# A decoder trunk on one core: chunks share first-projection weights, squares are summed in pairs, convolution taps are laid out anew, the norms' order is fixed, and half of the normed tiles stay in PSUM

## The chip, the cores and the metric

The kernel runs on one core of a Trainium2 chip. The metric is the device time of one execution in microseconds (us), given as the median of several runs. TensorE (PE in the rows) has a granted clock of 1.0 (2.4 GHz) or 0.5 (1.2 GHz) in the rows. VectorE is DVE, ScalarE is ACT, GpSimd is POOL, and SyncE is SP, which issues the DMAs.

## What is computed

The whole trunk is one launch, for 1024 tokens of width 1024 in float32:

```python
for layer in range(2):
    if layer == 0:   h = h + conformer_conv(h, ...)
    else:            h = h + nsa_attention(h, ..., kv)
    h = h + swiglu_ffn(h, ...)                 # (silu(gate) * up) @ w_out, behind an rmsnorm
    if layer == 0:   kv = shared_kv(h, ...)    # keys and values, computed once
return rmsnorm(h, final_norm)

def conformer_conv(x, ...):
    a, b = split(rmsnorm(x) @ pw1_w + pw1_b, 2)          # first projection
    h = a * sigmoid(b)
    h = depthwise causal convolution of 31 taps (h) + dw_b
    h = silu(layernorm(h))
    return h @ pw2_w + pw2_b                             # second projection
```

Attention takes softmax(score - slope * distance), with a mask, over three branches (compressed, selected and window), weighted by gates.

## The kernel before

The tokens are held in two chunks, c = 0 and 1, of 512 each (T), and each of the 1024 columns lies on partitions, in 8 tiles (KT) of 128x512. Matrix products keep float32 accuracy by three matmuls: each operand is split into a high part (yh, wh) and a low part (yl, wl), and `mm3` (L137) issues wh·yh, wh·yl and wl·yh for each of the 8 tiles k. A split (L177, L179) is a copy on ACT (yh) and a subtraction on DVE or POOL (yl). Weights come by one DMA of 512 KB, a copy on ACT (L158) and a subtraction on POOL (L160).

**First projection.** `pw1_tile(c, j)` fills two PSUM tiles, the value and its gate, with 24 matmuls each; `pw1_out` multiplies both by the norm's factor in chunk 0 (L361, L362), and makes u (L371) from the gate's tanh. So the norm's factor comes after the projection in chunk 0, and ahead of it in chunk 1 (`norm_y`, L272, makes the normed tile, and the split follows).

**Convolution.** Each tile of u has 31 taps. n1 of them go through ACT (product cv, L328) and POOL (sum zb, L329), n2 through PE as a diagonal matrix dgw (L319, L320, two passes each), and DVE takes the rest, one instruction each (L332), into a PSUM tile. The sum with zb is z (L336), and z is added up over the tiles in acc (L343).

**Norms.** Squares are added up on DVE or POOL into one tile acc (L190), and four column matmuls with ones (L201, in pieces called statistics below) give the sums of squares. Ten DVE instructions on 128x4 (L252 to L262) take the inverse root, a diagonal dg (L213) is made of it, and one matmul with ones (L220) spreads it over the partitions. The layernorm takes the mean first (`centre`, L382), and its squares of chunk 0 aren't added up: each of the eight goes to four statistics of its own. `normal` multiplies z (L401), takes the silu on ACT (L403) and splits.

**What sets the order.** PE's order is written by hand. `go(g, time)` runs the generator g of matmuls for so long, and `sides` holds the statistics, one of which goes behind each matmul of `mm3`. The tiles of the first projection of chunk 1 are the filler `fill` that PE runs while the layernorm of chunk 0 and the norm behind it are worked out. The other engines' orders come from a scheduler; `behind(g, rate)` runs the convolution beside the main generator, and `mark` and `later` add edges of order. Each engine runs its own list in order. PSUM has 8 banks here for `mm_ps()`, of one tile each; normed tiles lie in them where `roomy` is set, and so take the banks that the next matmuls need.

```python
        for k in range(KT):
            t = self.mm_ps() if self.roomy and k not in pool else self.tmp("yt")
            nc.vector.scalar_tensor_tensor(t, self.h[c][k], ..., r, OP.mult, OP.mult)
            y.append(split(t, k) if split else self.split(t, "pool" if k in pool else "dve"))
```

Of the kernel before, what the change touches and what calls it, by code (L numbers as in the profile page):

```python
# [37 lines left out]
NEG = -1e30  # L38
# [36 lines left out]
TAPS = (9, 4), (10, 0)  # L75
TAPS_END = (5, 6)
# [4 lines left out]
RATE0 = 1.05  # L81
# [17 lines left out]
PRINT = 0  # L99
YB = 16  # L100


class Net:
# [23 lines left out]
    def mm3(self, ps, w, y, kts, start=True, stop=True):  # L127
# [6 lines left out]
        for a, k in enumerate(kts):  # L134
            yh, yl = y[k]
            for b, (x, y_) in enumerate(((wh, yh), (wh, yl), (wl, yh))):
                nc.tensor.matmul(ps, x[:, a, :], y_, start=start and a + b == 0,  # L137
                                 stop=stop and a == n - 1 and b == 2)
                if self.sides:
                    self.sides.pop(0)()  # L140
# [32 lines left out]
    def split(self, src, lo="dve"):  # L173
# [3 lines left out]
        nc.scalar.activation(yh, src, AF.Copy)  # L177
# [4 lines left out]
    def sumsq(self, c, k, src, eng, pool=None):  # L182
# [4 lines left out]
        else:  # L187
            sq = pool.tile([128, T], F32, name="sq", tag="b") if pool else self.tmp("sq")
            nc.scalar.activation(sq, src, AF.Square)
            eng.tensor_tensor(self.acc[c], self.acc[c], sq, OP.add)  # L190
# [74 lines left out]
    def norm_y(self, c, vcol, split=None, pool=(), kept=False):  # L265
# [3 lines left out]
        y = []  # L269
        for k in range(KT):  # L270
            t = self.mm_ps() if self.roomy and k not in pool else self.tmp("yt")
            nc.vector.scalar_tensor_tensor(t, self.h[c][k], self.vec[:, vcol + k:vcol + k + 1],  # L272
                                           r, OP.mult, OP.mult)
            y.append(split(t, k) if split else self.split(t, "pool" if k in pool else "dve"))
        return y
# [15 lines left out]

    def later(self, ins):
# [9 lines left out]
    def conv_tile(self, c, j):  # L302
# [5 lines left out]
        n1, n2 = TAPS_END if c == 0 and j == KT - 1 else TAPS[c]  # L308
# [28 lines left out]
        if j == 0:  # L337
            self.acc[c] = z
        else:
            old = self.acc[c]  # L340
            if j == 1:
                self.acc[c] = self.cp.tile([128, T], F32, name="acc", tag="acc", bufs=2)
# [10 lines left out]
    def pw1_out(self, c, j, r=None):  # L353
# [5 lines left out]
        a = self.tmp("a")  # L359
        if r is not None:  # L360
            nc.vector.tensor_tensor(th, pb, r, OP.mult)  # L361
            nc.vector.tensor_tensor(a, pa, r, OP.mult)  # L362
            pa, pb = a, th
# [5 lines left out]
        else:  # L369
            nc.scalar.activation(u[:, 0:CW - 1], self.u[c - 1][j][:, T:T + CW - 1], AF.Copy)  # L370
        nc.vector.scalar_tensor_tensor(u[:, CW - 1:], th, 1.0, a, OP.add, OP.mult)  # L371
        self.u[c][j] = u

    def pw1_tile(self, c, j, r=None):
        yield from self.pw1_mm(c, j, self.y[c])
        self.pw1_out(c, j, r)

# [16 lines left out]
    def normal(self, c):  # L394
# [4 lines left out]
        y = []  # L399
        for j in range(KT):  # L400
            self.later(nc.vector.tensor_tensor(z[j], z[j], r, OP.mult))  # L401
            s = self.tmp("si") if c or j in LNP[c] else self.mm_ps()
            nc.scalar.activation(s, z[j], AF.Silu, bias=self.vec[:, V_LNB + j:V_LNB + j + 1],  # L403
                                 scale=self.vec[:, V_LNG + j:V_LNG + j + 1])
            y.append(self.split(s, "pool" if j in LNP[c] else "dve"))
        if c == 0:
            self.mark(self.last)
        self.yln[c] = y

    def layernorm(self, c):  # L410

        yield 4.0
        self.centre(c)
        yield 10.0
        self.sides.extend(self.rstd_parts([self.acc[c]]))
        yield 6.0
        while self.sides:
            yield 1.0
        self.rstd_spread(c, True)
# [408 lines left out]
    def q_tile(self, j, c):  # L828
# [4 lines left out]
        for g in range(2):  # L833
            a = slice(g * DH, (g + 1) * DH)
            b = slice((1 - g) * DH, (2 - g) * DH)
            f = DH ** -0.5 / SLOPE[g * HG + j]
# [65 lines left out]
    def bias_base(self):  # L902
# [3 lines left out]
        for (c0, w, step, off) in ((0, S, 1, 896), (BT_WIN, 640, 1, 512),  # L906
                                   (BT_CMP, 119, 16, 896 - (LC - 1))):
            nc.gpsimd.iota(b[:, c0:c0 + w], pattern=[[step, w]], base=-off,
                           channel_multiplier=-1, allow_small_or_imprecise_dtypes=True)
            nc.gpsimd.affine_select(out=b[:, c0:c0 + w], in_=b[:, c0:c0 + w],  # L910
                                    pattern=[[-step, w]], compare_op=OP.is_ge, fill=NEG,
                                    base=off, channel_multiplier=1)
        nc.gpsimd.affine_select(out=b[:, BT_WIN:BT_WIN + 640], in_=b[:, BT_WIN:BT_WIN + 640],
                                pattern=[[1, 640]], compare_op=OP.is_ge, fill=NEG,
# [34 lines left out]
    def scores(self, out, K, q, g, head, i, win):  # L949


        nc = self.nc
# [18 lines left out]
        for a in range(m):  # L971
# [5 lines left out]
            for e, (br, p0, pn, b0) in enumerate(segs):  # L977
# [7 lines left out]
                init = mx[:, prev[e]:prev[e] + 1] if e in prev else -3.0e38  # L985
# [556 lines left out]
```

## Time and profile before

| | before |
|---|---|
| time, median of 3 runs | 2627.57 us (2625.74 to 2631.69) |
| the profiled execution: time, span | 2629.18 us, 2627.5 us |
| mean granted clock of TensorE | 0.981 |
| busy: PE, DVE, ACT, POOL | 2512.0 us (96%), 1765.8 us (67%), 1291.6 us (49%), 1469.2 us (56%) |
| PE matmuls | 12946 |
| weights of the first projection | 46 DMAs of 512 KB, those of the second projection included |

PE is busy nearly all of the span, so a gain must come from fewer matmuls, from its waits, or from the stretches at half clock. The profile's groups are sums over stages: the waits have to be looked up where they fall. A row of the timeline shows the start, the length, the engine, the line, output and inputs, and in brackets how long the engine was idle before it and what ended that.

### The profile page before, as it was taken

Reading aid. Unit: us, or ns where it says so; the run is one execution under the profiler, and the core shown is the slowest. Engines: PE = TensorE matmul, PEld = TensorE weight load, DVE = VectorE, ACT = ScalarE, POOL = GpSimd, SP = SyncE. Lnnn points to the kernel's source line nnn. Section 1 sums busy time; section 2 is a strip of 40 time slices with the busy share of each in tenths; the row PEclk is TensorE's granted clock in tenths of the full one; section 3 lists DMA queues with packets and bytes.
Section 4 is the critical chain, followed back from the end, with each engine's and each line's share of the span. In section 5 each row is a group of like instructions: output and inputs, shape, how many; then the busy total and the mean of one; then the engine's idle time right before and its main releaser. Section 6 shows DMA issues by size and latency. Waiting matters only on the chain. (4 is left out here: it accounts for less than half of the span.)

```text
span 2627.5 us, 37191 instructions
## 1 busy us (share of the span) xinstructions
PE 2512.0 (96%) x12946; PEld 2083.5 (79%) x12946; DVE 1765.8 (67%) x3652; ACT 1291.6 (49%) x2517; POOL 1469.2 (56%) x1156
## 2 busy tenths in 40 slices
PE   8898899999799999999999999999999999899997
PEld 6676788888677878887878788888888887698986
DVE  6995788677774556665556566667666655777775
ACT  6555554444534554555543355555555543334444
POOL 8794889666543554555543354535445433566664
PEclk9999899999899999999999999999999999999999
DMA  4222223232446222322355531213212124143332
GB/s 163 72 73 66 80 81 97 88 93 92 152 146 190 87 89 62 112 86 82 90 161 167 190 101 45 81 44 108 70 53 74 54 78 158 58 129 97 97 95 75
DMA packets 111212, 258.29 MB, mean 98 GB/s; under 512 B 17265, under 2 KB 28848, under 8 KB 111024
## 3 DMA queue, kind: packets, MB, share of 16 engines
q1 hardware_dynamic: 111024, 255.91, 31.0%
q8 instruction: 102, 1.67, 0.3%
q14 instruction: 86, 0.70, 0.1%
HBM read 226.37 MB, written 29.42 MB: 97 GB/s over the span
## 5 line engine op out<-in xcount | busy, mean ns | idle before, releaser
L160 POOL TENSOR_TENSOR wl<-wr,wh 128x1024 fp32r<-128x1024 f32 (+2 forms) x396 | 740.6, 1872 | 661.1 <-ACT wh L158 625.1
L137 PE MATMUL mm<-yh,wh 128*128 128x512 f32 x1424 | 595.4, 418 | 31.7 <-DVE yl L179 30.4
L137 PE MATMUL mm<-yl,wh 128*128 128x512 f32 x1424 | 567.6, 399 | 5.0 <-DVE yl L179 5.0
L137 PE MATMUL mm<-yh,wl 128*128 128x512 f32 x1424 | 566.2, 398 | 1.8 <-POOL wl L160 1.8
L158 ACT ACTIVATE wh<-wr 128x1024 fp32r<-128x1024 f32 (+2 forms) x396 | 332.5, 840 | 426.3 <-PE mm L137 287.1
L137 PE MATMUL mm<-gh,wh 128*128 128x512 f32 x1360 | 439.4, 404 | 1.8 <-ACT gh L592 1.4
L137 PEld LDWEIGHTS mm<-yh,wh 128*128 128x128 f32 x1424 | 272.1, 191 | 86.3 <-DVE yl L179 32.1
L137 PEld LDWEIGHTS mm<-yh,wl 128*128 128x128 f32 x1424 | 271.3, 191 | 63.5 <-POOL wl L160 2.2
L137 PEld LDWEIGHTS mm<-yl,wh 128*128 128x128 f32 x1424 | 272.6, 191 | 49.5 <-DVE yl L179 6.2
L1030 DVE TENSOR_TENSOR pl<-pt,ph 128x512 fp32r<-128x512 f32 (+3 forms) x320 | 206.4, 646 | 149.6 <-ACT ph L1029 148.7
L137 PEld LDWEIGHTS mm<-gh,wh 128*128 128x128 f32 x1360 | 243.3, 189 | 48.8 <-issue 3.5
L137 PE MATMUL mm<-gh,wl 128*128 128x512 f32 x680 | 270.0, 397 | 3.7 <-POOL wl L160 3.7
L1029 ACT ACTIVATE ph<-pt 128x512 fp32r<-128x512 f32 (+3 forms) x320 | 178.7, 559 | 177.6 <-PE pt L1026 175.2
L1000 POOL TENSOR_SCALAR PS<-PS,sm,gates 128x31 f32<-128x31 f32 (+9 forms) x256 | 154.7, 615 | 191.4 <-DVE sm L997 164.6
L332 DVE SCALAR_TENSOR_TENSOR mm<-u,vec,mm 128x512 f32<-128x512 f32 x306 | 225.6, 752 | 8.0 <-PE mm L320 1.8
L995 ACT ACTIVATE PS<-PS,mx 128x31 f32<-128x31 f32 (+9 forms) x256 | 139.5, 546 | 115.6 <-DVE mx L993 115.3
L329 POOL TENSOR_TENSOR zb<-zb,cv 128x512 f32<-128x512 f32 x132 | 178.8, 1355 | 14.4 <-ACT zb L314 8.8
L1000 POOL TENSOR_SCALAR PW<-PW,sm,gates 128x640 f32<-128x640 f32 (+4 forms) x128 | 96.2, 752 | 155.1 <-DVE sm L997 131.8
L606 DVE TENSOR_TENSOR h<-mm,h 128x512 f32<-128x512 f32 x184 | 124.7, 684 | 81.7 <-PE mm L137 81.3
L137 PEld LDWEIGHTS mm<-gh,wl 128*128 128x128 f32 x680 | 128.0, 188 | 37.7 <-POOL wl L160 7.5
L995 ACT ACTIVATE PW<-PW,mx 128x640 f32<-128x640 f32 (+4 forms) x128 | 88.8, 694 | 101.2 <-DVE mx L993 100.5
L507 PE MATMUL mm<-y,wh 128*128 128x256 f32 x1008 | 133.8, 286 | 2.3 <-DVE wh L492 1.9
(243 smaller groups left out, 4814.4 us busy)
## 6 DMA issues: line engine op xcount, KB each, us to landing
wr<-in_fin_dram SPq DMA_DIRECT2D x176, 512.0 KB, 3.3
wr<-in_fout_dram SPq DMA_DIRECT2D x128, 256.0 KB, 2.7
wr<-in_pw_dram SPq DMA_DIRECT2D x46, 512.0 KB, 3.3
wr<-in_fout_dram SPq DMA_DIRECT2D x64, 192.0 KB, 2.4
wr<-in_wq_dram SPq DMA_DIRECT2D x16, 512.0 KB, 4.0
qd<-q SPq DMA_DIRECT2D x32, 256.0 KB, 2.2
qt<-qd SPq DMA_DIRECT2D x32, 256.0 KB, 2.8
wr<-in_wo_dram SPq DMA_DIRECT2D x16, 512.0 KB, 3.7
```

Of the source, the lines that this page charges most:

```text
L137: nc.tensor.matmul(ps, x[:, a, :], y_, start=start and a + b == 0, stop=stop and a == n - 1 and b == 2)
L158: nc.scalar.activation(wh[:, :kt, :cols], wr[:, :kt, :cols], AF.Copy)
L160: e.tensor_tensor(wl[:, :kt, :cols], wr[:, :kt, :cols], wh[:, :kt, :cols].bitcast(F32), OP.subtract)
L329: nc.gpsimd.tensor_tensor(zb, zb, t, OP.add)
L332: later(nc.vector.scalar_tensor_tensor(ps, u[:, w:w + T], dw(w), ps, OP.mult, OP.add))
L507: nc.tensor.matmul(ps, u[:, a], v, start=a + b == 0, stop=a == n - 1 and b == 2)
L606: self.nc.vector.tensor_tensor(h, ps, h, OP.add)
L995: nc.scalar.activation(P[:, p0:p0 + pn], P[:, p0:p0 + pn], AF.Exp, bias=mx[:, e:e + 1], accum_out=sm[:, e:e + 1])
L1000: nc.gpsimd.tensor_scalar(P[:, p0:p0 + pn], P[:, p0:p0 + pn], sm[:, e:e + 1], self.gates[:, i, gt:gt + 1], OP.mult, OP.mult)
L1029: nc.scalar.activation(ph[:rows, :width], pt[:rows, :width], AF.Copy)
L1030: nc.vector.tensor_tensor(pl[:rows, :width], pt[:rows, :width], ph[:rows, :width].bitcast(F32), OP.subtract)
```

## The change

- Tiles j = 4 to 7 of the first projection load their weights once for both chunks (`pw1_pair`); chunk 1 is then taken in the order 4, 5, 6, 7, 3, 2, 0, 1.
- In the first two norms squares are added in pairs on POOL (three pairs, and two tiles alone: 5 tiles, 20 statistics in place of 4); those of the first norm go back to back on PE, not between matmuls. The layernorm of chunk 0 has 20 statistics in place of 32. In eight other norms the last squared tile ("sl") isn't added but gets 4 statistics of its own. In all there are 128 statistics, 76 before.
- PE's taps (dgw) go from 34 to 22; POOL's products go from 132 to 140; DVE's taps go from 306 to 310.
- `pw1_out` works in place in PSUM. A copy of each tile's last 30 columns (halo) is kept for chunk 1.
- `norm_y` puts only even tiles into PSUM, and edges of order hold a multiplication back until the split of two tiles before is done (AHEAD); `normal` gets such edges as well.
- In the attention the scores' sign is turned, so that 256 small DVE instructions (TENSOR_SCALAR on 128x1 or 128x2) fall away.

```diff
-TAPS = (9, 4), (10, 0)
-TAPS_END = (5, 6)
+TAPS = (10, 2), (10, 0)
+TAPS_FIRST, TAPS_END = (11, 0), (5, 10)
-RATE0 = 1.05
+RATE0 = 0.85
+AHEAD = 2
+WARM = 4.0
+ORDER1 = (4, 5, 6, 7, 3, 2, 0, 1)
...
+    def paired(self, sq):
+        for k in range(0, KT - 2, 2):
+            self.nc.gpsimd.tensor_tensor(sq[k], sq[k], sq[k + 1], OP.add)
+        return sq[0:KT - 2:2] + sq[KT - 2:]
...
-        self.sides.extend(self.rstd_parts(tiles or [self.acc[c]]))
+        self.sides.extend(self.rstd_parts(tiles or [self.acc[c], self.sq[c]]))
...
-            t = self.mm_ps() if self.roomy and k not in pool else self.tmp("yt")
+            t = self.mm_ps() if self.roomy and k % 2 == 0 and k not in pool else self.tmp("yt")
...
+            if len(low) >= AHEAD:
+                self.order(ins, low[-AHEAD])
...
-            nc.vector.tensor_tensor(th, pb, r, OP.mult)
-            nc.vector.tensor_tensor(a, pa, r, OP.mult)
-            pa, pb = a, th
+            nc.vector.tensor_tensor(pb, pb, r, OP.mult)
+            nc.vector.tensor_tensor(pa, pa, r, OP.mult)
...
+    def pw1_pair(self, j):
+        w = self.wload(self.pw1[j], 8), self.wload(self.pw1[8 + j], 8)
+        for c in range(NC):
+            yield from self.pw1_mm(c, j, self.y[c], w)
+            self.pw1_out(c, j, None if c else self.rs[0])
...
+            if len(low) > AHEAD:
+                self.order(ins, low[-1 - AHEAD])
...
+            if len(high) >= AHEAD:
+                self.order(ins, high[-AHEAD])
...
-        self.rstd(1, g)
-        go(g, 2 * TILE)
+        g = pairs()
+        self.rstd(1, g, sq1)
         self.y[1] = self.norm_y(1, V_ANORM)
         go(g)
-        fill = every(self.pw1_tile, range(KT), 1)
-        go(fill, HOLD * 2 * TILE)
+        fill = every(self.pw1_tile, ORDER1[KT - 4:], 1)
+        go(fill, 4 * TILE)
         self.rest()
-        go(fill, 2.0)
         sq = self.centre(0)
-        go(fill, 6.0)
-        self.rstd(0, fill, sq)
+        go(fill, WARM)
+        self.per = 2
+        self.rstd(0, fill, self.paired(sq))
+        self.per = 1
```

At three places this is what the engines' lists become. The first is DVE at the layernorm of chunk 0, from the first product z·r on. Before, all eight products stand ahead of the first split (mm_1875 and so on are silu tiles in PSUM):

```order
L401 TENSOR_TENSOR z_414<-z_414,mm_1872 128x512
L401 TENSOR_TENSOR z_550<-z_550,mm_1872 128x512
...
L401 TENSOR_TENSOR z_1295<-z_1295,mm_1872 128x512
L401 TENSOR_TENSOR z_1427<-z_1427,mm_1872 128x512
L179 TENSOR_TENSOR yl_1878<-mm_1875,yh_1877 128x512
L179 TENSOR_TENSOR yl_1885<-mm_1882,yh_1884 128x512
L179 TENSOR_TENSOR yl_1892<-mm_1889,yh_1891 128x512
```

After the change, at the same place:

```order
L442 TENSOR_TENSOR z_427<-z_427,mm_1891 128x512
L442 TENSOR_TENSOR z_651<-z_651,mm_1891 128x512
L442 TENSOR_TENSOR z_799<-z_799,mm_1891 128x512
L183 TENSOR_TENSOR yl_1897<-mm_1894,yh_1896 128x512
L442 TENSOR_TENSOR z_951<-z_951,mm_1891 128x512
L183 TENSOR_TENSOR yl_1904<-mm_1901,yh_1903 128x512
L442 TENSOR_TENSOR z_1086<-z_1086,mm_1891 128x512
L183 TENSOR_TENSOR yl_1911<-mm_1908,yh_1910 128x512
L442 TENSOR_TENSOR z_1250<-z_1250,mm_1891 128x512
L183 TENSOR_TENSOR yl_1918<-mm_1915,yh_1917 128x512
```

Products and splits now alternate. PE's filler waits for the split yl_1892 (the third) before and for yl_1918 (the fourth) after.

The second place is DVE at the norm ahead of the keys and values of chunk 0 (V_KVN), six products into PSUM before, with four of the next norm (yt) behind them and ahead of the splits:

```order
L272 SCALAR_TENSOR_TENSOR mm_6305<-h0_97,vec_88,mm_6277 128x512
L272 SCALAR_TENSOR_TENSOR mm_6311<-h0_98,vec_88,mm_6277 128x512
L272 SCALAR_TENSOR_TENSOR yt_6695<-h0_93,vec_88,rs_6279 128x512
L272 SCALAR_TENSOR_TENSOR yt_6700<-h0_94,vec_88,rs_6279 128x512
L272 SCALAR_TENSOR_TENSOR yt_6705<-h0_95,vec_88,rs_6279 128x512
L272 SCALAR_TENSOR_TENSOR yt_6710<-h0_96,vec_88,rs_6279 128x512
```

After the change:

```order
L292 SCALAR_TENSOR_TENSOR mm_6245<-h0_94,vec_88,mm_6241 128x512
L292 SCALAR_TENSOR_TENSOR yt_6251<-h0_95,vec_88,mm_6241 128x512
L199 TENSOR_TENSOR acc_6193<-acc_6193,sq_6297 128x512
L183 TENSOR_TENSOR yl_6248<-mm_6245,yh_6247 128x512
L292 SCALAR_TENSOR_TENSOR mm_6257<-h0_96,vec_88,mm_6241 128x512
L183 TENSOR_TENSOR yl_6254<-yt_6251,yh_6253 128x512
L292 SCALAR_TENSOR_TENSOR yt_6263<-h0_97,vec_88,mm_6241 128x512
L183 TENSOR_TENSOR yl_6260<-mm_6257,yh_6259 128x512
```

Four tiles lie in PSUM in place of eight, the first split is the fourth instruction, and the next norm's products come behind the last split.

The third place is PE at the norm ahead of the first feed-forward network (chunk 0). Before, 17 filler matmuls (some of them are shown) stand between the last statistic (L201) and the spread (L220), and 27 behind it:

```order
L201 MATMUL mm_2356<-ones_86,acc_2034 128x1
L137 MATMUL mm_2376<-yl_895,wh_2365 128x512
L137 MATMUL mm_2376<-yh_894,wl_2366 128x512
...
L137 MATMUL mm_2376<-yl_925,wh_2365 128x512
L137 MATMUL mm_2376<-yh_924,wl_2366 128x512
L220 MATMUL mm_2416<-dg_2397,ones_86 128x512
L137 MATMUL mm_2376<-yh_930,wh_2365 128x512
```

After the change the spread (L240) follows the statistics (L221), and the network's own matmuls follow it:

```order
L221 MATMUL mm_2374<-ones_86,acc_2053 128x1
L140 MATMUL mm_1887<-yl_581,wh_1881 128x512
L221 MATMUL mm_2374<-ones_86,acc_2053 128x1
L140 MATMUL mm_1887<-yh_580,wl_1882 128x512
L221 MATMUL mm_2374<-ones_86,acc_2053 128x1 x2
L221 MATMUL mm_2374<-ones_86,sl_2355 128x1 x4
L240 MATMUL mm_2405<-dg_2403,ones_86 128x512
L140 MATMUL mm_2467<-yh_2409,wh_2456 128x512
```

The filler has been used up by then.

## Rows read from the trace of the kernel before

**Rows 1.** Waits of PE: line waited for, us in total, times, longest us.
```profile
PE mm L137 <- DVE yl L179: 35.4, 7, 10.2
PE mm L201 <- DVE acc L190: 10.6, 3, 5.0
```

**Rows 2.** PE's timeline, the matmul behind each long wait of the first 730 us.
```profile
80.46 1.12 PE L220 MATMUL mm<-dg,ones 128*128 128x512 f32 x2 [2.50 <-DVE dg L213]
...
109.93 0.80 PE L137 MATMUL mm<-yh,wh 128*128 128x512 f32 x1 [6.42 <-DVE yl L179]
...
242.97 0.79 PE L137 MATMUL mm<-yh,wh 128*128 128x512 f32 x1 [10.23 <-DVE yl L179]
...
296.67 0.38 PE L201 MATMUL mm<-ones,acc 128*128 128x1 f32 x2 [2.89 <-DVE acc L190]
...
312.46 0.80 PE L137 MATMUL mm<-yh,wh 128*128 128x512 f32 x1 [5.29 <-DVE yl L179]
...
703.54 0.59 PE L201 MATMUL mm<-ones,acc 128*128 128x1 f32 x2 [4.98 <-DVE acc L190]
...
723.09 0.80 PE L137 MATMUL mm<-yh,wh 128*128 128x512 f32 x1 [8.49 <-DVE yl L179]
```

**Rows 3.** Windows at half clock behind these waits (busy us, PEclk 0.50).
```profile
105.91:116.15 10.24, 6.22 (x15) 4.87 (x16) 10.24 (x16) 4.46 (x9) 9.85 (x7) 0.50 0.22 72
235.62:245.86 10.24, 2.89 (x7) 2.31 (x8) 5.02 (x9) 8.97 (x16) 8.60 (x6) 0.50 0.18 54
297.06:303.88 6.83, 6.83 (x20) 5.57 (x21) 3.58 (x12) 2.06 (x3) 4.69 (x3) 0.50 0.45 152
310.71:317.54 6.83, 5.08 (x12) 4.02 (x13) 6.83 (x11) 3.71 (x7) 4.73 (x4) 0.50 0.25 79
703.24:710.07 6.83, 6.53 (x19) 5.51 (x20) 3.34 (x13) 1.57 (x2) 4.43 (x2) 0.50 0.60 192
716.90:727.14 10.24, 4.05 (x10) 3.18 (x11) 10.24 (x16) 3.33 (x7) 1.74 (x1) 0.50 0.37 128
```

**Rows 4.** Timeline of ACT and DVE, layernorm of chunk 0: silu, second split, high parts.
```profile
233.64 1.47 ACT L403 ACTIVATE mm<-z,vec 128x512 f32<-128x512 f32 x2
...
241.04 0.69 DVE L179 TENSOR_TENSOR yl<-mm,yh 128x512 fp32r<-128x512 f32 x1 [4.69 <-ACT yh L177]
...
241.61 2.98 ACT L177 ACTIVATE yh<-mm 128x512 fp32r<-128x512 f32 x6
```

**Rows 5.** DVE's timeline at the norm V_KVN of chunk 0.
```profile
706.73 0.17 DVE L252 TENSOR_SCALAR mm<-mm 128x4 f32<-128x4 f32 x1 [0.32 <-PE mm L201]
...
708.73 0.69 DVE L213 TENSOR_TENSOR dg<-ident,mm 128x512 f32<-128x512 f32 x1
713.87 4.05 DVE L272 SCALAR_TENSOR_TENSOR mm<-h,vec,mm 128x512 f32<-128x512 f32 x6 [4.46 <-ACT rs L229]
```

**Rows 6.** PE's statistics between matmuls, and PE's taps from 41 to 202 us.
```profile
68.64 0.39 PE L137 MATMUL mm<-yh,wh 128*128 128x512 f32 x1
68.86 0.28 PE L201 MATMUL mm<-ones,acc 128*128 128x1 f32 x2
...
69.31 0.28 PE L201 MATMUL mm<-ones,acc 128*128 128x1 f32 x2
...
L320 PE MATMUL mm<-u,dgw 128*128 128x512 f32 x64 | 29.9, 601 | 4.4 <-ACT dgw L319 4.4
```

**Rows 7.** Convolution of chunk 0: a window (PE, PEld, DVE, ACT, POOL busy), the mean's matmul.
```profile
100.00:125.00 25.00, 18.43 (x60) 12.97 (x59) 24.75 (x37) 12.87 (x22) 17.57 (x12) 0.80 0.20 66
...
201.66 1.02 PE L382 MATMUL mm<-acc,ones 128*128 128x512 f32 x2
```

**Rows 8.** DVE's groups, by shapes, of the whole span (busy us, mean ns).
```profile
L179 DVE TENSOR_TENSOR yl<-yt,yh 128x512 fp32r<-128x512 f32 x30 | 32.3, 1109 | 0.1
L371 DVE SCALAR_TENSOR_TENSOR u<-th,a 128x512 f32<-128x512 f32 x16 | 19.2, 1197 | 12.8 <-PE mm L201 7.4 <-ACT a L365 5.3
...
L332 DVE SCALAR_TENSOR_TENSOR mm<-u,vec,mm 128x512 f32<-128x512 f32 x306 | 225.6, 752 | 8.0 <-PE mm L320 1.8
```

More of the change, by code (lines that the diff above doesn't have):

```diff
@@ L138, in mm3 @@
                                  stop=stop and a == n - 1 and b == 2)
-                if self.sides:
-                    self.sides.pop(0)()
+                for _ in range(self.per):
+                    if self.sides:
+                        self.sides.pop(0)()
             if a == 2:
@@ L187, in sumsq, with squares @@
         else:
-            sq = pool.tile([128, T], F32, name="sq", tag="b") if pool else self.tmp("sq")
+            if k < KT - 1:
+                sq = self.tmp("sq")
+            else:
+                sq = self.sq[c] = self.cp.tile([128, T], F32, name="sl", tag="rs", bufs=2)
             nc.scalar.activation(sq, src, AF.Square)
-            eng.tensor_tensor(self.acc[c], self.acc[c], sq, OP.add)
+            if k < KT - 1:
+                eng.tensor_tensor(self.acc[c], self.acc[c], sq, OP.add)
+    def squares(self, src, pool):
+        sq = pool.tile([128, T], F32, name="sq", tag="b")
+        self.root = self.nc.scalar.activation(sq, src, AF.Square)
+        return sq
+    def paired(self, sq):
+        for k in range(0, KT - 2, 2):
+            self.nc.gpsimd.tensor_tensor(sq[k], sq[k], sq[k + 1], OP.add)
+        return sq[0:KT - 2:2] + sq[KT - 2:]
     def rstd_parts(self, tiles):
@@ L268, in norm_y @@
         r = self.rs[c] if kept else self.rp[c]
-        y = []
+        y, low = [], []
         for k in range(KT):
-            t = self.mm_ps() if self.roomy and k not in pool else self.tmp("yt")
-            nc.vector.scalar_tensor_tensor(t, self.h[c][k], self.vec[:, vcol + k:vcol + k + 1],
-                                           r, OP.mult, OP.mult)
+            t = self.mm_ps() if self.roomy and k % 2 == 0 and k not in pool else self.tmp("yt")
+            ins = nc.vector.scalar_tensor_tensor(
+                t, self.h[c][k], self.vec[:, vcol + k:vcol + k + 1], r, OP.mult, OP.mult)
+            if kept:
+                self.later(ins)
+            if len(low) >= AHEAD:
+                self.order(ins, low[-AHEAD])
             y.append(split(t, k) if split else self.split(t, "pool" if k in pool else "dve"))
+            if not split and k not in pool:
+                low.append(self.last)
         return y
@@ L289, in blocks7, with order @@
             yield
+    def order(self, ins, old):
+        self.tc.add_manual_dep(ins.ins, old.ins.name, mybir.DependencyInfo(
+            mybir.DependencyClass.NoSync, mybir.DependencyReason.DATA))
     def later(self, ins):
@@ L1266, in run @@
         self.nraw = 0
-        self.off, self.bg, self.marks, self.sides = [], None, {}, []
+        self.off, self.bg, self.marks, self.sides, self.per = [], None, {}, [], 1
+        self.halo = self.tp.tile([128, KT, CW - 1], F32, name="halo", tag="halo", bufs=1)
         self.h = [[self.hp.tile([128, T], F32, name="h0", tag="h", bufs=8) for k in range(KT)],
@@ L1297, in conv @@
         def conv(c):
-            for j in range(KT):
-                while (j + 1 not in self.u[c] if j + 1 < KT else
-                       c == 0 and 0 not in self.u[1]):
+            for j in ORDER1 if c else range(KT):
+                while (j if c else min(j + 1, KT - 1)) not in self.u[c]:
                     yield 0.5
@@ L1310, in every, with pairs @@
                 yield from f(c, n, *a)
-        def raw_tiles():
-            for j in range(2, KT):
+        def pairs():
+            for j in (2, 3):
                 yield from self.pw1_tile(0, j, self.rs[0])
+            for j in range(4, KT):
+                yield from self.pw1_pair(j)
         go = self.go
@@ L1444, in run @@
         self.y[1] = self.norm_y(1, V_KVN)
+        self.mark(self.last)
         go(g)
```

78 lines of the change are left out of this document (46 added, 32 removed).

## Prediction

> **What bounds it now.** I read the table first: PE is busy 96% of the span, so what can be won lies in PE's waits, in the half-clock stretches behind them, or in matmuls that fall away. The waits by releaser come next: 35.4 us for the low part of a split in seven waits, 10.6 us for a sum of squares in three [rows 1]. The timeline says where: all the longest ones but one (the third for a sum, below) lie before 730 us, at the norms around the convolution of chunk 0, at the layernorm, and at the norm V_KVN [rows 2]. The reader should see that the matmul behind the wait at 232 to 243 us is a filler (yh, wh of the first projection), whose operands are long there. What it lacks is a PSUM bank: normed or silu tiles hold the banks, and one comes free only with a split. Why the split is late: DVE's list has eight products ahead of the first split, and ACT mixes the silus with copies for the convolution, so that DVE's second split starts only at 241.04, after 4.69 us idle for ACT's high part [rows 4]. At V_KVN six multiplications run from 713.87 on for 4.05 us [rows 5], four of the next norm stand behind them in DVE's list, and only then come the splits for which PE waits until 723.09 [rows 2].
>
> Each such wait also drops the granted clock from 1.0 to 0.5. The windows give what that costs: the half of PE's busy time in them, 3.1, 1.4, 3.4, 2.5, 3.3 and 2.0 us in order [rows 3].
>
> During the convolution of chunk 0 DVE is the busier engine: 24.75 of 25 us [rows 7]. So PE's gains there can be taken back by DVE.
>
> **The change part by part**, against the profiled execution of 2629.2 us.
>
> *Prices.* A matmul takes 68.86 - 68.64 = 0.22 us (0.227 over a run), and a statistic with a matmul 69.31 - 68.86 = 0.45, so a statistic is 0.23 [rows 6]. A tap of PE: 29.9 us for 64 passes, 32 taps, 0.93 each, and 4.4 us of waits for their matrices (same rows). A tap of DVE: 0.752; u from SBUF operands 1.197; a split from SBUF 1.109 [rows 8], against 0.69 from PSUM [rows 4].
>
> *Up to the mean of chunk 0* (matmul L382 at 201.66 [rows 7]). PE loses 12 taps, -11.2 us, and half of the waits for their matrices, -2.2. The first two norms get 16 statistics each, 32 x 0.23 = +7.4. The wait of 2.50 us for dg goes, since the 20 statistics of the second norm are taken earlier in the filler: -2.5. The norm of chunk 1, 6.42 of wait and 3.1 of clock, has four tiles in PSUM, not eight, and chunk 1's matmuls come later: I leave 1 us of it, -8.5. Sum -17.0. PE also does 75 filler matmuls more ahead of the mean, 75 x 0.227 = 17.0 us, so it could reach L382 where it stands now, at 201.7, with 17 us of later work done. But DVE has four taps more (+3.0), four splits from SBUF (+1.7), and 13 u from PSUM, at about a tap's 0.75, in place of 11 at 1.197 (-3.4): about +1.3 on an engine that is full, with pauses for statistics and for filler results that I can't read from before. From nothing (201.7) to 10 us (212) late; I take 206, as DVE's own sum is nearest to the lower end. Gain 17.0 - 4.3 = 12.7; bounds 6.7 and 17.
>
> *Layernorm of chunk 0.* 10.23 of wait and 1.4 of clock. Now products and splits alternate, and the filler waits for the fourth split. From the spread on, ACT needs 1.47/2 + 2.98/6 = 1.23 us for silu and high part of a tile [rows 4], so the fourth split ends some 7 us behind it (a product of 0.7, four times 1.23, a split of 0.7, and hops), and PE has 21 + 3 filler matmuls, 5.5 us. Then 9 more and the second projection, which takes a tile in 0.68 us where ACT gives one in 1.23. I leave 4 us of wait and 2 of clock: -5.6. Twelve statistics fewer: -2.7. Together -8.3; bounds 0 (a fourth split as late as the third was) and -14.
>
> *Norm of the first network, chunk 0.* Now 2.89 + 5.29 of wait and 3.4 + 2.5 of clock, 14.1. The wait for the last sum goes, as the last square isn't added. But the filler ends here: the inverse root and dg, 706.73 to 709.42 or 2.7 us [rows 5], with hops on both sides some 3.7, have no cover any more, and then the network's matmuls take tiles (0.68 each) as fast as DVE multiplies and splits them (4.05/6 for the product [rows 5], 0.69 or 1.109 for the split: 1.4 to 1.8): 2 + 7 x 0.9 = 8.3. With 3.4 of clock 15.4, and 4 statistics, 0.9: +2.2. Bounds -4 and +8.
>
> *V_KVN of chunk 0.* 4.98 + 8.49 of wait and 3.3 + 2.0 of clock, 18.8. One addition of two SBUF tiles on DVE goes from the first wait, which I price as u, 1.2 [rows 8]; 3.8 and its clock stay. The second: DVE's first split is now fourth in its list, and PE has three filler tiles, 3 x 24 x 0.227 = 16 us, before it needs a bank; the wait goes with its clock. -11.7, and +0.9 for statistics: -10.8. Bounds -1 and -16.
>
> *The rest.* Six more norms with four statistics: 24 x 0.23 = +5.5. The third wait for a sum, 10.6 - 2.89 - 4.98 = 2.7 us [rows 1, 2], loses an addition: -1.2. So +4.3. The 256 small instructions in the attention lie on DVE, which is 67% busy in all, beside a PE without waits that name it in [rows 1]: nothing; a stall behind them could give up to some us, which I leave to the range. The shared weights take eight DMAs and eight splits off SP, ACT and POOL: nothing, since no wait of rows 1 names a weight.
>
> Sum: -12.7 - 8.3 + 2.2 - 10.8 + 4.3 = -25.3, so 2603.9 as profiled, and 1.6 less against the median of the runs: **2602 us**.
>
> **Rivals.**
> *A. DVE takes it back.* The convolution ends when DVE does; with the pauses at 10 us or more, and the first network's norm at its upper bound, 2602 + 6 + 6 = 2614, up to 2620. For: 24.75 of 25 [rows 7]. Against: the added sum is 1.3. Chance 0.17.
> *B. Splits from SBUF are slow.* Eleven splits and multiplications now lie in SBUF. At 1.109 they cost 0.42 more each [rows 4, 8]; if where POOL is busy each takes twice that, the uncovered ones, five at the first network's norm and four at chunk 1's, add 9 x 1 us: 2611. The Trainium skill, "SBUF — State Buffer", section "SBUF: two separate sides", has the rule that speaks against the change: a DVE operation with two SBUF inputs and a GpSimd operation that reads SBUF take a shared port in turn, each blocked for the other's whole length. The spread between 1.109 and 0.69 agrees with it in sign. Chance 0.10.
> *C. Slower.* One mechanism: PE's hand-written list takes 75 filler matmuls into the convolution, and each pair of tiles needs two banks that only `pw1_out` frees, through a DVE that is behind with taps. PE then stands still, and DVE's taps behind PE's taps with it. It decides where L382 comes after 201.7 + 26 + 4 = 232 us, as the whole gain is then gone. For it: DVE's list is in order. Against: DVE would have to pause for 30 us of 160. With L382 at 240: 2636. Chance 0.09.
> *D. The clock stays up.* No half-clock stretch at the layernorm and the first network's norm (2 + 3.4), nor at V_KVN's first wait (3.3), and half of the waits that I leave there (4 + 3.8): 2602 - 12.6 = 2589, down to 2583. Chance 0.10.
> *E. No change that shows*: the waits move behind the next bank, V_KVN at its lower bound (+10), the layernorm at its own (+8) and A's 6: 2626. Chance 0.06.
>
> **How the numbers follow.** My own case has the rest, 0.48, from 2594 to 2612. A to E take the range to 2585 to 2624, which leaves C, half of E and a part of D outside, under 2 in 10. 0.2% is 5.3 us, about what a measurement of this kernel can tell from no change. Faster: own, A, B, D and a little of E, 0.85; same: most of E, 0.06; slower: C, 0.09.
>
> **What would show it.** Right: the matmul behind V_KVN's spread without a wait of 8 us; the layernorm's wait under 5; no wait at the norm of chunk 1; L382 between 202 and 212 us; at the first network's norm a wait for dg of 3 us or more; 22 taps and 128 statistics of PE. The waits for yl in all at half of 35.4. Wrong: L382 after 215, a wait for yl of 8 us anywhere before 730, or a difference in the attention's stretch, where I expect none.

## The result, and the profile after

| | before | changed |
|---|---|---|
| median | 2626.65 us (4 runs) | 2585.57 us (4 runs, 2583.31 to 2586.79) |
| profiled span | 2627.5 us | 2584.0 us |

The ratio is 0.9841, with a 95% interval of 0.9824 to 0.9858: 41 us faster. I had said 2602, so the direction was right and the gain was 1.6 times what I forecast; it lies at the lower edge of the range.

The profiled execution after, by engine and by PE's waits (us in total, times, longest):

```profile
PE 2506.5 (97%) x13026; PEld 2093.0 (81%) x13026; DVE 1686.7 (65%) x3392; ACT 1294.4 (50%) x2513; POOL 1444.8 (56%) x1151
...
PE mm L140 <- DVE yl L183: 9.2, 6, 4.7
...
PE mm L240 <- DVE dg L233: 6.4, 3, 3.2
...
PE mm L140 <- DVE h L479: 4.9, 1, 4.9
PE mm L351 <- ACT dgw L350: 4.2, 1, 4.2
...
PE mm L221 <- DVE acc L199: 1.7, 1, 1.7
PE mm L221 <- POOL sq L209: 1.7, 1, 1.7
```

The reader should see that the waits for yl went from 35.4 to 9.2 us, and those for a sum of squares from 10.6 in three to 1.7 in one [rows 1]; a wait of 1.7 for a pair of squares that POOL adds is new. PE's busy time fell by 5.5 us, from 2512.0 to 2506.5, and its idle time by 38.0, from 115.5 to 77.5: the gain is nearly all waiting. PE's timeline at the places of [rows 2] and one new one:

```profile
208.22 0.59 PE L422 MATMUL mm<-acc,ones 128*128 128x512 f32 x1
...
241.81 0.76 PE L140 MATMUL mm<-yh,wh 128*128 128x512 f32 x1 [4.69 <-DVE yl L183]
...
298.48 2.08 PE L240 MATMUL mm<-dg,ones 128*128 128x512 f32 x2 [3.24 <-DVE dg L233]
302.04 0.80 PE L140 MATMUL mm<-yh,wh 128*128 128x512 f32 x1 [1.48 <-ACT yh L181]
...
487.64 0.50 PE L558 MATMUL mm<-y,wl 128*128 128x256 f32 x2 [1.29 <-DVE y L504]
492.24 1.52 PE L558 MATMUL mm<-y,wl 128*128 128x256 f32 x3 [4.10 <-ACT y L503]
...
693.68 0.38 PE L221 MATMUL mm<-ones,acc 128*128 128x1 f32 x2 [1.68 <-DVE acc L199]
...
740.11 0.77 PE L140 MATMUL mm<-yh,wh 128*128 128x512 f32 x1 [4.88 <-DVE h L479]
```

The mean of chunk 0 comes at 208.22, 6.6 us later than before, with 75 filler matmuls more done ahead of it. The wait for chunk 1's norm is gone, the layernorm's is 4.69 (10.23 before), and the first network's norm has its uncovered dg, 3.24 + 1.48. Two waits of 1.3 and 4.1 us are new, at 486 to 492 us in the second layernorm. At V_KVN the wait for a bank is gone; PE later waits 4.88 for h.

Stretches at half clock have moved rather than gone. Five of those in the changed kernel, with the columns of [rows 3]:

```profile
24.71:34.95 10.24, 10.24 (x38) 9.08 (x38) 2.34 (x11) 4.84 (x7) 8.08 (x6) 0.50 0.50 191
178.31:185.14 6.83, 5.15 (x6) 2.01 (x7) 4.36 (x7) 4.00 (x8) 6.45 (x5) 0.50 0.21 77
219.27:229.51 10.24, 10.24 (x36) 8.89 (x36) 2.35 (x11) 0.00 (x0) 0.00 (x0) 0.50 0.07 26
...
297.77:308.01 10.24, 7.57 (x14) 4.52 (x15) 8.07 (x12) 4.32 (x7) 5.01 (x4) 0.50 0.16 54
488.92:495.75 6.83, 3.36 (x14) 3.07 (x15) 5.29 (x7) 2.75 (x6) 4.33 (x4) 0.50 0.35 115
```

The first, the second, the third and the last are new. Half of PE's busy time in a stretch, as in the prediction, puts them at 5.1, 2.6, 5.1 and 1.7 us; the one at the first network's norm costs 3.8. The mean granted clock is 0.982, and was 0.981.

How far the changed kernel is ahead, by the same instruction in both (the spread of a norm, or the first and last score matmul of an attention stage):

| place | before, us | changed, us | gain in the stretch | forecast |
|---|---|---|---|---|
| spread of V_KVN, chunk 0 | 712.18 | 700.85 | 11.3 | 18 |
| first score of attention 0 | 858.35 | 836.72 | 10.3 | 10 |
| last score of attention 0 | 1321.24 | 1295.23 | 4.4 | 0 |
| first score of attention 1 | 1524.45 | 1492.30 | 6.1 | loss of 1 |
| last score of attention 1 | 2131.68 | 2091.62 | 7.9 | 0 |
| end of the span | 2627.5 | 2584.0 | 3.4 | loss of 2 |

(The forecast's terms are put to the stretches where they fall.) The surprise is in the attention, 12.3 us, and in the later norms, 9.5 us won in two stretches where I had expected a loss of 3. Ahead of V_KVN the change gained less than forecast. A place is good to some 5 us only: experiments 2 and 3 below have the changed kernel's code up to the attention, and their first score comes at 836.38 and 841.56.

### The profile page after: what moved, and what is told of

It is laid out like the page before. It is cut to its first block, busy times and chain, and to the rows that moved or that the text cites. A ratio compares the mean times of both kernels' runs of the same rounds, so it can differ in the third digit from the quotient of the medians.

```text
span 2584.0 us, 37109 instructions
## 1 busy us (share of the span) xinstructions
PE 2506.5 (97%) x13026; PEld 2093.0 (81%) x13026; DVE 1686.7 (65%) x3392; ACT 1294.4 (50%) x2513; POOL 1444.8 (56%) x1151
## 4 chain that ended last, share of the span: by engine, by line
PE 74%; DVE 15%; DMA 4%; issue 3%; ACT 2%; POOL 2%; SPq 0%; DVEq 0%; ACTq 0%; POOLq 0%
PE mm L140 52%; PE po L1102 6%; PE sc L1027 5%; PE pt L1077 5%; PE mm L558 3%; DVE mm L363 3%; DMA wr<-in_fin_dram 1%; DMA wr<-in_fout_dram 1%; POOL wl L164 1%; DVE yt L292 1%; DVE wh L543 1%; PE mm L221 1%; DVE yl L183 1%; DVE acc L199 1%; DVE ws L533 1%
## 5 line engine op out<-in xcount | busy, mean ns | idle before, releaser
L164 POOL TENSOR_TENSOR wl<-wr,wh 128x1024 fp32r<-128x1024 f32 (+2 forms) x388 | 718.3, 1853 | 640.0 <-ACT wh L162 613.6
L140 PE MATMUL mm<-yh,wh 128*128 128x512 f32 x1424 | 594.6, 418 | 12.3 <-DVE h L479 4.9
L162 ACT ACTIVATE wh<-wr 128x1024 fp32r<-128x1024 f32 (+2 forms) x388 | 324.1, 835 | 385.9 <-PE mm L140 238.9
L140 PE MATMUL mm<-yP,wh 128*128 128x512 f32 (+1 forms) x416 | 134.7, 402 | 0.0
```

Source lines behind the costliest of these rows:

```text
L162: nc.scalar.activation(wh[:, :kt, :cols], wr[:, :kt, :cols], AF.Copy)
L164: e.tensor_tensor(wl[:, :kt, :cols], wr[:, :kt, :cols], wh[:, :kt, :cols].bitcast(F32), OP.subtract)
```

## The experiments

The edits stand against the changed kernel or the kernel before, as each says; ratios are to the kernel before, so 0.9841 is the changed kernel's. Differences in us are between medians; the ratios put them up to 3 us higher or lower. A line ... in an edit stands for lines left out.

**1. The attention's sign alone, in the kernel before.** 256 negations go, as the sign is turned (in the scale of the queries, the distances and the mask as well).

```diff
-                    SLOPE[head], init, OP.add, OP.max, mx[:, col:col + 1])
+                    SLOPE[head], init, OP.add, OP.min, mx[:, col:col + 1])
...
-        nc.vector.tensor_scalar(mx[:, :ns], mx[:, :ns], -1.0, None, OP.mult)
-            nc.scalar.activation(P[:, p0:p0 + pn], P[:, p0:p0 + pn], AF.Exp,
+            nc.scalar.activation(P[:, p0:p0 + pn], P[:, p0:p0 + pn], AF.Exp, scale=-1.0,
```

> The kernel before with the turned sign of the scores alone, so that the 256 small DVE instructions of the attention go. Theory (each of them stands in the chain from the reduction to the exponential, and PE ends up waiting for it): about 13 us faster than before, 2614, all of it between the first and the last score matmul of the two attention stages (4.5 and 8). Rival (as I predicted: no cost, and the attention's gain of the whole change has another origin, such as the earlier start or the place of weight loads): no change, 2627 within 3.

Measured 2611.42, ratio 0.9937 (0.9922 to 0.9952). The theory holds. PE's and DVE's busy time in the two attention stages, from the windows of before and of this kernel (the columns are those of [rows 3]):

```profile
858.00:1321.20 463.20, 460.21 (x2320) 376.77 (x2319) 271.28 (x886) 245.51 (x625) 243.81 (x272) 1.00 0.29 85
1524.40:2131.70 607.30, 602.26 (x3223) 505.41 (x3223) 408.81 (x1231) 342.14 (x712) 290.34 (x270) 1.00 0.22 67
```

```profile
854.00:1312.50 458.50, 458.50 (x2318) 377.09 (x2317) 244.01 (x763) 249.41 (x626) 243.88 (x272) 1.00 0.28 86
1513.40:2111.90 598.50, 598.01 (x3222) 506.08 (x3221) 379.24 (x1109) 348.15 (x717) 291.67 (x271) 1.00 0.23 68
```

The same 5540 or so matmuls take 4.7 and 8.8 us less. PE's idle time was 3.0 and 5.0 us and is now nothing and 0.5; the other 6 of the 13.5 us are less busy time for the same work at the same clock, and what makes it was not told apart. The profiled execution gained 18.9 us in all; the rest lies at places that the edit doesn't touch, 3.7 between the first network's norm and V_KVN's spread and 2.4 between the attention stages, which is within the scatter of such places.

**2. The sign as before, in the changed kernel** (the same lines the other way round).

> The changed kernel with the scores' sign as before, so that the 256 small instructions are back. Theory: 13 us slower than the changed kernel, 2598 to 2599. Rival (another origin of the attention's gain): 2586 within 3.

Measured 2603.07, ratio 0.9904 (0.9885 to 0.9923): 17.5 us slower than the changed kernel. The two attention stages take as long as in the kernel before, within 0.4 us.

**3. The same small instructions aside.** They run where the negations ran on DVE, but nobody waits for them.

```diff
         ns = len(segs)
+        dm = self.sm.tile([128, 2], F32, name="dm", tag="dm", bufs=4)
+        nc.vector.tensor_scalar(dm[:, :ns], mx[:, :ns], -1.0, None, OP.mult)
```

> The changed kernel with 256 small DVE instructions of the same kind and at the same places of DVE's list, which write a tile that nobody reads. If it is the chain (the exponential waits for the negation) that costs: no change against the changed kernel, 2586 within 3. If it is DVE's time (256 x 0.15 to 0.2 us = 45 us more busy, other splits late): as slow as with the sign turned back, about 2598.

Measured 2593.24, ratio 0.9863 (0.9847 to 0.9880): in between. The stages take 461.2 and 600.8 us:

```profile
841.60:1302.80 461.20, 459.07 (x2318) 376.85 (x2317) 273.06 (x890) 249.98 (x626) 244.44 (x272) 1.00 0.29 86
1500.00:2100.80 600.80, 598.35 (x3223) 506.18 (x3222) 405.24 (x1232) 348.66 (x716) 292.10 (x271) 1.00 0.23 68
```

The changed kernel takes 458.5 and 599.3. So of the 12.3 us some 4 are DVE's time and 8 the chain, in which the exponential waits for the negation. (34 of the 256 negations stand in DVE's list of experiment 2 right behind a reciprocal, which needs ACT's exponential before it; what share these have was not measured.) PE's waits at the end of this chain, first of the kernel before and then of this one:

```profile
PE po L1051 <- DVE pl L1030: 3.4, 9, 0.7
...
PE pt L1026 <- POOL PS L1000: 2.3, 4, 1.5
...
PE po L1051 <- ACT ph L1029: 1.9, 2, 1.3
```

```profile
PE po L1104 <- DVE pl L1083: 3.1, 4, 1.5
...
PE sc L1027 <- DVE mx L1039: 0.9, 1, 0.9
...
PE pt L1079 <- POOL PS L1053: 0.6, 1, 0.6
```

**4. The second layernorm's pauses as before.**

```diff
-        yield 10.0
+        yield 4.0
         self.centre(c)
-        yield 16.0
+        yield 10.0
...
-        yield 1.0
+        yield 6.0
         while self.sides:
             yield 1.0
-        yield 14.0
         self.rstd_spread(c, True)
```

> The changed kernel with the pauses of the second layernorm as before (4, 10, 6, none, in place of 10, 16, 1, 14). Theory (the new waits of 1.3 and 4.1 us near 486 to 492 us and the half clock behind them, some 8 us together, come from the layernorm falling together with the blocks of the next network's operands): the waits go, 2578 to 2582. Rival (the collision comes from the convolution's end, whatever the pauses): the wait stays or moves, 2586 within 3, or slower if the filler between statistic and spread is missed.

Measured 2598.18, ratio 0.9886 (0.9871 to 0.9901): 13 us slower, so the theory fell in its sign. The two waits did go, but a longer one came, since without the pause of 14 the spread follows the statistics with little time for the inverse root. So this run doesn't tell what the place of the layernorm is worth:

```profile
492.97 2.07 PE L240 MATMUL mm<-dg,ones 128*128 128x512 f32 x2 [8.46 <-DVE dg L233]
```

**5. The rmsnorm's products as before, in the changed kernel.**

```diff
-            t = self.mm_ps() if self.roomy and k % 2 == 0 and k not in pool else self.tmp("yt")
+            t = self.mm_ps() if self.roomy and k not in pool else self.tmp("yt")
...
-            if len(low) >= AHEAD:
-                self.order(ins, low[-AHEAD])
...
```

> The changed kernel with the rmsnorm's multiplications as before: all tiles in PSUM where there is room, and no edges of order in it. Theory (the long waits at the norm of chunk 1 and at V_KVN were PSUM banks held by tiles that aren't split): they come back, about 8.5 at the first and 5 to 10 at V_KVN, 10 to 18 us slower than the changed kernel, 2596 to 2604. Rival (the banks aren't what holds PE, since chunk 1's matmuls now come later and cover the splits anyway): 2586 within 4.

Measured 2599.58, ratio 0.9892 (0.9875 to 0.9908): 14 us slower, as the theory has it. The waits are back at chunk 1's norm, the first network's and V_KVN. The edit takes the edges of order out as well, but experiment 12 takes only edges out and loses nothing, so banks were what held PE:

```profile
63.40 0.77 PE L140 MATMUL mm<-yh,wh 128*128 128x512 f32 x1 [5.17 <-DVE yl L183]
...
303.32 0.76 PE L140 MATMUL mm<-yh,wh 128*128 128x512 f32 x1 [5.55 <-DVE mm L292]
...
718.11 0.79 PE L140 MATMUL mm<-yh,wh 128*128 128x512 f32 x1 [9.90 <-DVE yl L183]
```

**6. The new products alone, in the kernel before** (the edit of 5 the other way round).

> The kernel before with the new multiplications of the rmsnorm alone (even tiles in PSUM, edges of order). Theory: the waits of 6.4, 5.3 and 8.5 us with their half clock shrink, 12 to 22 us faster than before, 2606 to 2616. Rival (the wait is taken over by the next split, or by splits from SBUF beside POOL): under 5 us, 2623 to 2628.

Measured 2621.23, ratio 0.9971 (0.9960 to 0.9982): 7 us faster, between the two. Two waits moved rather than shrank, one to a tap of PE and one to h; the layernorm's, the second of these rows, the edit leaves as it was:

```profile
118.86 1.22 PE L332 MATMUL mm<-u,dgw 128*128 128x512 f32 x1 [9.26 <-ACT dgw L331]
...
246.50 0.79 PE L138 MATMUL mm<-yh,wh 128*128 128x512 f32 x1 [10.23 <-DVE yl L180]
...
751.14 0.77 PE L138 MATMUL mm<-yh,wh 128*128 128x512 f32 x1 [6.37 <-DVE h L440]
```

**7. The taps as before, in the changed kernel.**

```diff
-TAPS = (10, 2), (10, 0)
-TAPS_FIRST, TAPS_END = (11, 0), (5, 10)
+TAPS = (9, 4), (10, 0)
+TAPS_FIRST, TAPS_END = (9, 4), (5, 6)
```

> The changed kernel with the convolution's taps of chunk 0 as before (9 on ACT and POOL, 4 on PE, 18 on DVE; 34 taps of PE in all). As I predicted, PE gets 12 taps more, 11.2 us with waits for their matrices of some 2, on a PE that now ends the convolution 2 us behind DVE: 9 to 14 us slower than the changed kernel, 2595 to 2600. Rival (DVE with 4 taps fewer and POOL with 8 sums fewer give it back): 2586 within 4.

Measured 2606.78, ratio 0.9919 (0.9900 to 0.9938): 21 us slower, nearly all of it ahead of the mean of chunk 0, which comes at 227.48:

```profile
76.72 2.07 PE L351 MATMUL mm<-u,dgw 128*128 128x512 f32 x2 [7.39 <-ACT dgw L350]
...
227.48 0.70 PE L422 MATMUL mm<-acc,ones 128*128 128x512 f32 x1
```

**8. The last square added again, in the changed kernel.**

```diff
-            if k < KT - 1:
-                sq = self.tmp("sq")
-            else:
-                sq = self.sq[c] = self.cp.tile([128, T], F32, name="sl", tag="rs", bufs=2)
+            sq = self.tmp("sq")
             nc.scalar.activation(sq, src, AF.Square)
-            if k < KT - 1:
-                eng.tensor_tensor(self.acc[c], self.acc[c], sq, OP.add)
+            eng.tensor_tensor(self.acc[c], self.acc[c], sq, OP.add)
...
```

> The changed kernel with the last square of the eight later norms added on DVE or POOL again, so 4 statistics in each, not 8. As I predicted (0.9 us a norm for statistics, 1.2 us a wait for the addition at three norms): 7 us less matmul work and some 4 us more waits, 2580 to 2584. Rival (statistics that PE takes while it waits for other things cost little, and the wait for the addition is longer with its half clock): the waits of 3 to 6 us ahead of the statistics come back, 2588 to 2598.

Measured 2592.71, ratio 0.9870 (0.9853 to 0.9887): 7 us slower, as the rival has it. The waits for a sum are back:

```profile
PE mm L217 <- DVE acc L195: 8.3, 3, 4.5
```

PE's busy time fell from 2506.5 to 2499.0, so 32 statistics cost 7.5 us as I had priced them; its idle time rose by 12.9. Only 2 us of the loss lie between the attention stages and behind them: of the three waits one falls there, 0.96 us.

**9. More filler behind the mean.**

```diff
-        go(fill, 4 * TILE)
+        go(fill, 3 * TILE)
```

> The changed kernel with one half tile, 24 matmuls or 5.4 us, of filler less ahead of the mean of chunk 0 and more behind it. Theory (the first network's norm has no cover: waits of 3.2 and 1.5 us there, and half clock behind them): they go, and since DVE ends the convolution 2 us ahead of PE, PE waits some 3 us at the mean: 2 to 6 us faster than the changed kernel, 2580 to 2584. Rival (the layernorm's wait or the mean's takes all of it back): 2586 within 3, or slower.

Measured 2598.86, ratio 0.9888 (0.9873 to 0.9902): 13 us slower. The wait for dg at the first network's norm went, and one for the convolution came. The waits in the second layernorm stayed, 5.9 us where the changed kernel has 5.4:

```profile
204.05 1.22 PE L422 MATMUL mm<-acc,ones 128*128 128x512 f32 x1 [3.21 <-DVE acc L375]
...
488.94 0.39 PE L558 MATMUL mm<-y,wl 128*128 128x256 f32 x1 [3.21 <-ACT y L503]
492.03 0.80 PE L558 MATMUL mm<-y,wl 128*128 128x256 f32 x2 [2.70 <-DVE y L504]
```

The mean came 4 us earlier than in the changed kernel, and V_KVN's spread, at 709.75, 9 us later. So the loss lies behind the first network's norm, and these waits explain a part of it only; the rest was not settled.

**10. The shared weights loaded twice, in the same order.**

```diff
-        w = self.wload(self.pw1[j], 8), self.wload(self.pw1[8 + j], 8)
         for c in range(NC):
+            w = self.wload(self.pw1[j], 8), self.wload(self.pw1[8 + j], 8)
```

> The changed kernel with the same order of matmuls, but the weights of tiles 4 to 7 loaded and split once for each chunk (eight more DMAs of 512 KB, eight more copies on ACT, eight more subtractions of 2.45 us on POOL). As I predicted: nothing, 2586 within 4. Rival (POOL is as full as DVE during the convolution, and its subtractions block DVE's operations on SBUF): 20 us of POOL more in a stretch of 150 put the mean of chunk 0 some 5 to 15 us later, 2591 to 2600.

Measured 2590.44, ratio 0.9861 (0.9846 to 0.9875). It is 5 us slower, with an interval that overlaps the changed kernel's; the profile has a wait of 5.40 us at 150.56 us, and the mean at 208.63, where the changed kernel has it. Small, just outside what I had said, and not the rival's 5 to 15 at the mean.

**11. The second layernorm later.**

```diff
-        yield 10.0
+        yield 30.0
         self.centre(c)
```

> The changed kernel with a pause of 30 in place of 10 ahead of the second layernorm's mean, so that its squares fall behind the blocks of the network's operands, not between them. Theory (the waits of 1.3 and 4.1 us at 486 to 492 and the half clock behind them are that collision): 5 to 8 us faster, 2578 to 2581. Rival (the blocks themselves, or the next thing that comes late, keep PE waiting): 2586 within 4.

Measured 2580.20, ratio 0.9823 (0.9808 to 0.9837): 5 us faster, as the theory has it. The interval overlaps the changed kernel's, but its four runs (2579.46 to 2581.45) all lie below the changed kernel's four. No wait of a microsecond is left between 464 and 516 us.

**12. Without the edges of order.**

```diff
-AHEAD = 2
+AHEAD = 99
```

> The changed kernel with half of the normed tiles in PSUM, but without the edges of order (products and splits as the scheduler likes, silus and high parts too). If the edges carry part of the gain: the layernorm's wait goes from 4.7 to 8 or 10 and V_KVN's splits come later, 5 to 12 us slower, 2591 to 2598. If the freed banks alone do it: 2586 within 4.

Measured 2582.90, ratio 0.9832 (0.9817 to 0.9846): not slower. The layernorm's wait is 4.61 without the edges and 4.69 with them, so the edges carry none of the gain:

```profile
238.02 0.80 PE L140 MATMUL mm<-yh,wh 128*128 128x512 f32 x1 [4.61 <-DVE yl L183]
```

**13. Edits 11 and 12 together.**

> The changed kernel with both of the edits that made it faster: the second layernorm's mean 30 units later, and no edges of order. If they lie at different places of the program and add up: 5.4 + 2.5 = 8 us faster than the changed kernel, 2577 to 2580. If the second only changed which wait falls where: 2580 to 2583, like the first alone.

Measured 2575.38, ratio 0.9792 (0.9776 to 0.9808), the fastest of all, 10 us ahead of the changed kernel and with an interval apart from its own: the two add up.

**14. The taps alone, in the kernel before** (the edit of 7 the other way round).

> The kernel before with the new layout of the taps alone (22 of PE, not 34). If PE's taps and the waits for their matrices are time by themselves, as undoing them in the changed kernel suggests (20 us): 13 to 20 us faster than before, 2607 to 2614. If DVE ends the convolution anyway while PE has little filler ahead of the mean: 0 to 4 us faster, 2623 to 2628, the mean's matmul at 200 to 203 us, and the 20 us are the taps and the moved filler together.

Measured 2629.98, ratio 1.0005 (0.9996 to 1.0015): nothing. With fewer taps PE waits longer for DVE, and the mean is later (209.71, and 201.66 before), not earlier:

```profile
109.35 0.79 PE L137 MATMUL mm<-yh,wh 128*128 128x512 f32 x1 [12.69 <-DVE yl L179]
...
209.71 1.02 PE L382 MATMUL mm<-acc,ones 128*128 128x512 f32 x2
```

**15. The last square alone, in the kernel before.** Eight norms get four statistics more, and an addition fewer (the edit of 8 the other way round).

> The kernel before with the last square of eight norms not added but given four statistics of its own. As undoing it in the changed kernel suggests: 6 to 9 us faster than before, 2619 to 2622, with the three waits for a sum of squares (2.9, 5.0 and 2.7) down to some 4 in all. As I predicted at first (32 more statistics, 7.3 us, against 1.2 us at each of three waits): 3 to 4 us slower, 2630 to 2632.

Measured 2613.07, ratio 0.9935 (0.9920 to 0.9950): 16 us faster, twice what the theory had and the other way than my first step:

```profile
PE mm L206 <- DVE acc L195: 2.8, 1, 2.8
```

The mean granted clock rose from 0.981 to 0.986 as well. Of PE's time, 13.8 us less are idle and 4.0 less busy, with 32 statistics more. The wait at V_KVN stays, now 9.90 us (8.49 before).

## Why the prediction was right in direction and short in size

**The steps that failed**, in the prediction's words: "The 256 small instructions in the attention ... nothing", which was 12.3 us, and in the later norms a wait that "loses an addition: -1.2", where the whole wait and the half clock behind it went, so that a forecast loss of 3 us was a gain of 9.5. Ahead of the attention errors of both signs cancel in part: 21.6 us measured, 28 forecast.

**Up to the mean: about right in the sum, in part by luck.** I forecast a gain of 12.7 and the mean at 206. It came at 208.22, so the stretch gained 17.0 - 6.6 = 10.4 us, within the bounds (205.78 and 206.18 in experiments 2 and 3, with the same code up to there). Inside it, the waits for the taps' matrices, of which half was to go, stayed: 4.2 us (4.4 before). The wait at chunk 1's norm went with its 3.1 of clock, but 5.1 and 2.6 us of half clock are new, and I had none there. The first of these stretches begins in the forty matmuls of 128x1 that the first norm takes back to back; the last wait of PE ahead of it is of 0.5 us. The second stands at the wait for the matrices. I priced PE's taps at 13.4 us and expected DVE to take back a part. Experiments 7 and 14 show that the taps have no price of their own: nothing in the kernel before, 21 us in the changed one. That with the filler moved ahead of the mean taps cost PE, and without it the time is DVE's, is how I read it; the filler was not undone by itself to this end.

**The layernorm: the wait right, the sum not.** I left 4 us of wait and 2 of clock, and 4.69 and some 2.4 stayed. But the statistics ahead of it got the wait of 1.67 us for POOL's pairs and the half clock from 219.27 on, together 6.8 us, where I had only 2.7 less for twelve statistics. Of the 8.3 us forecast next to nothing is left by these rows. Experiment 12 shows that the edges of order, to which I gave the shorter wait, do not matter; what lets PE wait less there was not told apart.

**The first network's norm: right in the wait for dg, wrong in the next term.** Expected was a wait for dg of 3 us or more, and 3.24 came. The 8.3 us of waits for tiles were 2.0 (1.48 and 0.48). At half clock PE takes a tile in 1.28 us (from 304.34 to 305.62), and the eight tiles came in 9.6, 1.2 each, so the slow clock and the wait cover one another, and I had added them. By these rows the norm costs 9.0 us, not 15.4, and 14.1 before.

**What was missed ahead of V_KVN.** The second layernorm got two new waits, 5.4 us together, with 1.7 us of half clock behind them. I had not looked at it, since I took its changed pauses as no more than timing. Experiment 11 moves it away from the next network's operand blocks, and the waits and 5 us go.

**V_KVN: about right.** From there to the attention it gained 10.3 us. Experiments 5, 6 and 12 show the mechanism, a bank held by a tile not yet split, and that it pays in full only beside the other changes: 14 us for all norms in the changed kernel, 7 in the kernel before.

**The later norms.** "Six more norms with four statistics: 24 x 0.23 = +5.5", less 1.2 for one addition, was to lose 4.3; the two stretches between the attention stages and behind them, where four of the six lie, gained 9.5. The statistics cost what I had said (experiment 8); the mis-sized term is the third wait for a sum. I took 1.2 of its 2.69 us off and left out the half clock behind it:

```profile
1379.08:1385.91 6.83, 6.83 (x21) 5.67 (x21) 3.03 (x12) 1.57 (x2) 4.33 (x2) 0.50 0.62 192
```

In the changed kernel PE has no wait at that norm and no half clock behind it, so 2.69 + 3.4 = 6.1 us went, as much as the stretch gained (its eight statistics cost 1.8, and its other waits give about as much). In experiment 15, the kernel before with the last square alone, that wait is gone too, and these two stretches gain 7.1 and 3.4. But experiment 8 loses only 2 us there: the addition then costs a wait of 0.96 us, and the clock stays up behind it. So in the changed kernel something else keeps the sum early as well. What that is, and what won the 3.4 us at the end, stays open.

**The attention.** "The 256 small instructions in the attention ... nothing" was 12.3 us in the profiles, 16 and 17.5 in experiments 1 and 2. I had named a difference in this stretch as a sign of being wrong, and it came. I argued from rows 1 that PE had no waits that name it. The full view of waits names three, 7.6 us together, none longer than 1.5 us, and I had sorted by the longest. Of the 12.3 us the chain has 8 and DVE's time 4 (experiment 3).

**The rivals.** C (slower) and E didn't happen. A did in experiment 14, in the kernel before. D's time came (2589 down to 2583), but not its mechanism: the clock did not stay up. B (slow splits from SBUF) did not. The rule of the Trainium skill, "SBUF — State Buffer", section "SBUF: two separate sides", was its ground. The trace agrees with the rule: the longest split from SBUF, 2.87 us, began 0.06 us behind a subtraction of POOL of 2.39 us and took that one's length and 0.5 us more. But my price of 1.109 was a mean of unlike splits. In the changed kernel those from SBUF took 1.013 us on average (1.109 before) and those from PSUM 0.682, yet half of those from SBUF took 0.68 too. The third of these rows has the shortest, the median and the longest in ns; the two behind it are of the timeline:

```profile
L183 DVE TENSOR_TENSOR yl<-yt,yh 128x512 fp32r<-128x512 f32 x41 | 41.4, 1013 | 0.8 <-ACT yh L181 0.4
L183 DVE TENSOR_TENSOR yl<-mm,yh 128x512 fp32r<-128x512 f32 x19 | 12.9, 682 | 3.0 <-ACT yh L181 3.0
L183 DVE TENSOR_TENSOR yl<-yt,yh x41: 676/679/2866, 61.7 to 2206.4; 128x512 fp32r<-128x512 f32 x41
...
2195.72 2.39 POOL L164 TENSOR_TENSOR wl<-wr,wh 128x1024 fp32r<-128x1024 f32 x1
2195.78 2.87 DVE L183 TENSOR_TENSOR yl<-yt,yh 128x512 fp32r<-128x512 f32 x1
...
L402 DVE SCALAR_TENSOR_TENSOR u<-th,mm 128x512 f32<-128x512 f32 x16 | 10.9, 682 | 8.5 <-ACT th L395 7.7 <-ACT mm L396 0.8
```

The eleven splits that the change puts into SBUF, all ahead of 715 us, took 0.68 to 1.12 us. The u from PSUM came at 0.682, better than the 0.75 that I took.

## What to carry to other kernels

A small instruction is not free because its engine has time to spare: ask what waits for it and what it waits for in its engine's list; many waits of half a microsecond add up as a long one does. Matmuls more on the busy engine are paid, but where they take the place of an addition for which it waits, the wait saved can be worth more (32 statistics more, 16 us less in experiment 15). A wait and a stretch at half clock at the same place can cover one another: look which of the two ends last before adding them. Parts of a change may be worth nothing alone and 21 us together, because another engine ends the stretch; undo a part in the new kernel and do it in the old one before giving it a price.

## What the runs showed that I had not expected

A wait of PE can cost more than its length: taking some 8 us of waits for sums of squares away (10.6 to 2.8) brought 16 us in experiment 15, while the mean granted clock rose from 0.981 to 0.986. Each of the three had a stretch of 6.83 us at half clock behind it in the kernel before. Other waits shrank too, so not all of the 16 us is shown to be theirs.

A stretch at half clock needn't stand right behind a long wait: the one from 24.71 to 34.95 us begins while PE takes matmuls of 128x1 one behind the other, and no wait in the 8 us before it is above 0.6 us.

The undoing of single parts sums to 17.5 + 21.2 + 14.0 + 7.1 + 4.9 = 64.7 us, more than the 41 of the whole.
